# Small products of a recurrent stage in one run per unit, sample products on the whole array, and a prompt stage whose first loads are asked for earlier

## The chip, the cores and the metric

The kernel runs on one core of one Trainium2 chip. The metric is the time of one execution in microseconds (us) on the device; of the kernel before it is 2415.64 us, the median of three runs.

## The reference

One inference step of a trunk layer for 2048 prompt tokens and 32 sample tokens (8 sequences of 4), 1024 channels wide. A norm and one input projection feed two branches; both are gated, projected back, merged and added to the input. Branch A is sparse attention (8 query heads, 2 key heads of 64) with a compressed, a selected and a sliding-window part. Branch B is a gated linear recurrence over 4 heads of 128 x 128 state, and it is what the change is about:

```
G = cumsum(log f)                      # per channel, within a chunk
A[t,s] = sum_d q[t,d] exp(G[t,d]-G[s,d]) k[s,d]   for s <= t
o[t]   = (q[t] exp(G[t])) S + sum_s A[t,s] v[s]
S      = exp(G_last) S + sum_s (k[s] exp(G_last-G[s]))^T v[s]
o      = o / rms(o) * norm_g * silu(z)
```

The sample tokens run the same recurrence from eight given states.

## The kernel before, in words

The kernel is one program whose instructions a scheduler orders on each engine, over the whole program, by what the code's order and the readiness of operands suggest; a block under `high_priority()` is taken ahead of what it would otherwise stand behind. The stages follow each other in the code: loading and compressing the prompt (to about 400 us), sample attention (to 600), the recurrent stage `hgrn` (640 to 1296), `attention_setup` and the preparation of the first two prompt blocks (to about 1386), and the prompt's attention blocks with the output projection (to the end). A generator of projection products is spread between them: `fill(ns)` issues so many ns of it, by a credit, after every step of a stage. Its products are those of L375 and L456 and, last, L435 (the gate columns, spread as 512- and 272-token products, written out to `mb_d` by L441); they are f16 and whole-array.

`hgrn` treats 32 units, eight chunks of 256 tokens by 4 heads, each chunk as two halves j of 128 tokens. A decay matrix within 128 tokens is made of products at five distances (`LEVELS` 64, 32, 16, 8, 4) and one for the nearest tokens. `factors` makes for each distance a factor tile X0 to X4 (a subtraction on DVE at L728, abs and exp on ACT at L729 and L730, two multiplies on POOL at L731 and L732), and the tiles Bk, Bq, Kd, Xo. `scores` multiplies them on PE in f32, by parts of the array: L751 one 64 x 64 product of X0 and two 32 x 32 of X1, L755 four 32 x 32 each of X2, X3, X4 and of Bk with Bq, for each j, 38 products a unit, into a PSUM tile `p4` for each j (two buffers). ACT and DVE gather them into AT (L758 to L766). `values` then makes the state's addend (L774), the outputs (L778 from AT, L780 from the state S) and the next S (L783, L785). `gate_out` scales, transposes (L659), gates and stores (L667, L668) four units at a time. `sample_heads` is put in as one step after each unit from the seventh on: 4 heads with tiles of 32 rows (products at L806, L811, L813, L818, L828, L838). A product in f32 shows as two records in the trace.

After the last unit `attention_setup` opens the pool `pc` (selected-key operands), makes scales, and loads `szs`, gates the sample outputs on DVE (L1410 to L1412) and stores them (L1413, L1414). Then `prompt_phase` opens its pools, asks for block 0's operands (L1500 to L1503), its window's keys (L1480 to L1485) and the selected keys, and prepares two blocks of two groups each: maxima (L1567), bias rows (L1445), scores (L1575, L1576), values (L1461 to L1464), selection on DVE (L1591 to L1599) and a transpose (L1603). All these loads are issued by the SP queue in order. A `pfill(2850.0)` after each step puts projection products between the steps. Pools on the right side of SBUF are stacked: a pool opened after another was closed takes its memory.

## Time and profile before

| | |
|---|---|
| median of three runs (lowest, highest) | 2415.64 us (2414.82, 2417.95) |
| the profiled execution | 2413.94 us |
| its span, first to last instruction | 2412.2 us |
| PE busy | 2279.5 us, 94% |
| DVE, ACT, POOL busy | 1533.5, 1182.3, 1021.4 us |
| mean granted TensorE clock | 0.980 of full speed |
| chain that ended last, by engine | PE 72%, DVE 11%, DMA 6%, ACT 4% |

An engine's busy time is the time in which at least one of its instructions is under way. PE is pipelined: many small products overlap, so the count of records times the mean of one is more than the busy time, and the distance of one start to the next is what a product costs. A run of like products is one row (`x20`); its length runs from the first start to the last end. `PEclk` is the granted TensorE clock in tenths or as a share of full speed. `[... <-DMA x]` behind a row is the engine's idle time before it and what ended it. The chain of waits and the waits of PE say which engine is waited for.

### The profile page before, as it was taken

Reading aid. Unit: us, or ns where it says so; the run is one execution under the profiler, and the core shown is the slowest. Engines: PE = TensorE matmul, PEld = TensorE weight load, DVE = VectorE, ACT = ScalarE, POOL = GpSimd, SP = SyncE. Lnnn points to the kernel's source line nnn. Section 1 sums busy time; section 2 is a strip of 40 time slices with the busy share of each in tenths; the row PEclk is TensorE's granted clock in tenths of the full one; section 3 lists DMA queues with packets and bytes.
Section 4 is the critical chain, followed back from the end, with each engine's and each line's share of the span. In section 5 each row is a group of like instructions: output and inputs, shape, how many; then the busy total and the mean of one; then the engine's idle time right before and its main releaser. Section 6 shows DMA issues by size and latency. Waiting matters only on the chain.

```text
span 2412.2 us, 56868 instructions
## 1 busy us (share of the span) xinstructions
PE 2279.5 (94%) x22181; PEld 1545.1 (64%) x22181; DVE 1533.5 (64%) x4088; ACT 1182.3 (49%) x2606; POOL 1021.4 (42%) x1184
## 2 busy tenths in 40 slices
PE   6999998999899998999989799899999999999998
PEld 5898775555685555556656456667677666665765
DVE  7555554756613689777774356768677677767543
ACT  5544332521422266555663256356556566667663
POOL 0000102242500056555550035356656567777764
PEclk9999999999999999999999899999999999999999
DMA  6643313676842443333332533432222221211121
GB/s 205 178 127 117 127 71 107 230 257 219 256 125 75 152 142 112 115 111 116 117 102 93 141 121 95 111 85 80 63 85 83 61 63 43 72 50 48 52 58 43
DMA packets 276109, 271.89 MB, mean 113 GB/s; under 512 B 102296, under 2 KB 246176, under 8 KB 268416
## 3 DMA queue, kind: packets, MB, share of 16 engines
q1 hardware_dynamic: 267328, 230.51, 31.2%
q0 software_dynamic: 8512, 37.75, 4.7%
q8 instruction: 174, 2.85, 0.5%
q14 instruction: 95, 0.78, 0.1%
HBM read 184.66 MB, written 87.74 MB: 113 GB/s over the span
## 4 chain that ended last, share of the span: by engine, by line
PE 72%; DVE 11%; DMA 6%; ACT 4%; issue 3%; SPq 2%; POOL 1%; ACTq 0%; POOLq 0%; DVEq 0%
PE ps L375 17%; PE ps L1809 7%; PE ps L1777 7%; PE ps L456 7%; PE ps L435 5%; PE st L1666 3%; PE st L1656 3%; PE mx L1536 3%; PE ph L969 2%; DVE X L728 2%; PE po L1461 2%; PE po L1462 2%; PE po L1464 2%; DMA wraw<-in_w_in_dram 1%; PE pt L952 1%
## 5 line engine op out<-in xcount | busy, mean ns | idle before, releaser
L1455 POOL TENSOR_TENSOR Pl<-P,Ph 128x512 f16<-128x512 f32 x444 | 522.1, 1186 | 316.6 <-ACT Ph L1454 178.6
L1453 ACT ACTIVATE P<-st 128x512 f32<-128x512 f32 x444 | 264.8, 597 | 239.8 <-PE st L1666 185.3
L375 PEld LDWEIGHTS <-wh 128*128 128x128 f16 x2240 | 216.0, 98 | 167.8 <-issue 16.2
L1454 ACT ACTIVATE Ph<-st 128x512 f16<-128x512 f32 x444 | 263.1, 595 | 10.5 <-PE po L1462 8.3
L375 PE MATMUL ps<-xh,wh 128*128 128x512 f16 (+1 forms) x1120 | 229.6, 342 | 4.7 <-DVE row L388 3.5
L375 PE MATMUL ps<-xh,wl 128*128 128x512 f16 (+1 forms) x1120 | 232.9, 343 | 0.0
L375 PE MATMUL ps<-xl,wh 128*128 128x512 f16 (+1 forms) x1120 | 231.7, 341 | 0.5 <-issue 0.5
L1539 DVE TENSOR_REDUCE mps<-mx 128x1 f32<-128x512 f32 (+3 forms) x320 | 185.8, 602 | 60.3 <-PE mx L1538 29.5
L456 PE MATMUL ps<-wh,xh 128*128 128x256 f16 (+1 forms) x680 | 190.3, 280 | 10.1 <-ACT to L464 4.8
L456 PE MATMUL ps<-wh,xl 128*128 128x256 f16 (+1 forms) x680 | 189.2, 279 | 4.1 <-DVE xl L341 4.1
L456 PE MATMUL ps<-wl,xh 128*128 128x256 f16 (+1 forms) x680 | 189.9, 279 | 0.0
L1461 PEld LDWEIGHTS <-Ph 128*128 128x128 f16 x1776 | 139.8, 98 | 39.5 <-ACT Ph L1454 5.2
L375 PEld LDWEIGHTS <-wl 128*128 128x128 f16 x1120 | 109.4, 99 | 83.1 <-issue 6.1
L456 PEld LDWEIGHTS <-xh 128*128 128x128 f16 x1360 | 131.1, 99 | 32.4 <-issue 7.7
L1462 PEld LDWEIGHTS <-Ph 128*128 128x128 f16 x1776 | 128.4, 97 | 32.6 <-issue 0.5
L697 POOL TENSOR_TENSOR Xo<-Xo,qt 128x256 f32<-128x256 f32 x32 | 33.3, 1041 | 260.7 <-ACT Xo L696 210.0
L1539 DVE TENSOR_REDUCE mpw<-mx 128x1 f32<-128x512 f32 (+3 forms) x224 | 102.8, 482 | 40.5 <-PE mx L1538 40.0
L1777 PEld LDWEIGHTS <-xh 128*128 128x128 f16 x1280 | 105.0, 98 | 32.7 <-issue 7.1
L731 POOL TENSOR_TENSOR X<-X,kt 128x128 f32<-128x128 f32 x160 | 91.5, 574 | 65.4 <-ACT X L730 63.0
L1464 PEld LDWEIGHTS <-Pl 128*128 128x128 f16 x1776 | 94.2, 97 | 25.9 <-POOL Pl L1455 8.8
L1461 PE MATMUL po<-vs,Ph 128*128 128x65 f16 x1088 | 105.5, 192 | 2.6 <-DVE otmp L1553 2.0
L1462 PE MATMUL po<-vs,Ph 128*128 128x64 f16 x1088 | 104.8, 193 | 0.0
(528 smaller groups left out, 5824.0 us busy)
## 6 DMA issues: line engine op xcount, KB each, us to landing
wraw<-in_w_in_dram SPq DMA_DIRECT2D x22, 1024.0 KB
xt<-in_x_prompt_dram SPq DMA_DIRECT2D x32, 512.0 KB
ma_d<-row SPq DMA_DIRECT2D x8, 1040.0 KB
out_y_prompt_dram<-xt SPq DMA_DIRECT2D x16, 512.0 KB
sg<-ma_d SPq DMA_DIRECT2D x56, 128.0 KB
sg<-mb_d SPq DMA_DIRECT2D x56, 128.0 KB
q_d<-row SPq DMA_DIRECT2D x4, 1040.0 KB
lf_d<-row SPq DMA_DIRECT2D x4, 1040.0 KB
```

The lines of the kernel that those rows point to most:

```text
L375: mm(ps, l[:, kc], xs(r, t0, n)[:, kc], k == 0, k == 23)
L435: mm(ps, l[:, kc, a * 128:(a + 1) * 128], xs(r, t0, n)[:, kc], k == 0, k == 23)
L456: mm(ps, x, w[:, kc], k == 0, k == 23)
L1453: ac.activation(P[:n], ps, AF.Exp, scale=1.0 / QS)
L1454: ac.activation(ph[:n], ps, AF.Exp, scale=1.0 / QS)
L1455: sub.tensor_sub(pl[:n], P[:n], ph[:n])
L1461: mm(po[:, r, :w], ph[:n, rs[r]], v[:n, :w], first and r == 0, False)
L1462: mm(po[:, r, :64], ph[:n, rs[r]], v[:n, w:w + 64], False, False)
L1464: mm(po[:, r, :w], pl[:n, rs[r]], v[:n, :w], False, last)
L1539: ve.tensor_reduce(mp_[:, r, c:c + 1], pmf[:, :n], axis=AX.X, op=OP.max)
L1777: mm(X["ps"], w[:, kc, cs], os_[o][:, kc], k == 0, k == 11)
L1809: mm(X["ps"], X["y"][y][:, kc, i0:i0 + r], W["o", kc // 4][w][:, kc % 4, cs], k == 0, k == 23)
```

## The change

Three things are changed in the code.

1. `scores` now issues all products of a unit, both halves j, in one loop under `high_priority()`, into one PSUM tile for both halves. Within a half X4 comes first, then Bk with Bq, X3, X2, X0, X1. The 64 x 64 product of X0 is written as two pieces of 32 columns by 64 tokens, so a unit has 40 products, all 32 wide, where it had 38.
2. The sample tiles with 32 rows or 32 columns are replaced by zeroed tiles of 128 (eight memsets on POOL when the stage begins), of which the first 32 are written. The products read the whole tiles. The last transpose of the samples becomes a product with the first 32 columns of the identity.
3. `prompt_phase` is a generator. It is opened before `attention_setup`: its pool `pu`, the memsets of XD and REP, block 0's loads and the window's loads stand ahead of `attention_setup` in the program; `pc` is opened later, in the first `load_keys`, and the PSUM pools after the generator is taken up again. The prompt's main part is then called from inside.

```diff
@@ -656,7 +656,10 @@
                 for j in range(nt):
-                    pe.transpose(pt[:, j * 128:j * 128 + r], o_sb[:r, j], ident[:r, :r])
+                    if r == 128:
+                        pe.transpose(pt[:, j * 128:j * 128 + r], o_sb[:, j], ident)
+                    else:
+                        mm(pt[:, j * 128:j * 128 + r], o_sb[:, j], ident[:, :r], True, True)
...
+            WIDE = {}
             def common(h, t0, n, L):
                 sfx = "" if n == NC else "_s"
                 def new(name, bufs=2):
+                    if n != NC and name in ("Bk", "Kd"):
+                        return WIDE[name][:, :n]
                     return hp.tile([128, n], F32, name=name + sfx, bufs=bufs if n == NC or name == "E" else 1)
@@ -739,25 +746,34 @@
+                p4 = pa.tile([128, 4, 128], F32, name="p4")
+                first = set()
+                for j in range(NJ):
+                    prod = []
+                    for li, (l, r) in reversed(list(enumerate([(x, x) for x in u["Xs"][2:]] + [(u["Bk"], u["Bq"])]))):
+                        for b in range(4):
+                            bs = slice(j * 128 + 32 * b, j * 128 + 32 * b + 32)
+                            prod.append((b, p4[32 * b:32 * b + 32, 2 * j + 1, 32 * li:32 * li + 32], l[:, bs], r[:, bs]))
+                    prod = prod[4:8] + prod[:4] + prod[8:]
+                    for li, L in enumerate(LEVELS[:2]):
+                        X = u["Xs"][li][:, j * 128:(j + 1) * 128]
+                        for s0 in range(0, 128, 2 * L):
+                            for c0 in range(s0, s0 + L, 32):
+                                prod.append((c0 // 32, p4[c0:c0 + 32, 2 * j, s0 + L:s0 + 2 * L], X[:, c0:c0 + 32], X[:, s0 + L:s0 + 2 * L]))
+                    with tc.high_priority():
+                        for b, o, l, r in prod:
+                            mm(o, l, r, b not in first, True)
+                            first.add(b)
                 u["AT"] = []
                 for j in range(NJ):
-                    tj = slice(j * 128, (j + 1) * 128)
-                    p4 = pa.tile([128, 4, 128], F32, name="p4")
-
-                    near = p4[:, 1].rearrange("p (l t) -> p l t", l=4)
-                    for li, L in enumerate(LEVELS[:2]):
-                        X = u["Xs"][li][:, tj]
-                        for s0 in range(0, 128, 2 * L):
-                            mm(p4[s0:s0 + L, 0, s0 + L:s0 + 2 * L], X[:, s0:s0 + L], X[:, s0 + L:s0 + 2 * L], li == 0 or s0 == 64, True)
-                    for li, (l, r) in enumerate([(x, x) for x in u["Xs"][2:]] + [(u["Bk"], u["Bq"])]):
-                        for b in range(4):
-                            bs = slice(j * 128 + 32 * b, j * 128 + 32 * b + 32)
-                            mm(near[32 * b:32 * b + 32, li], l[:, bs], r[:, bs], li == 0 and b == 3, True)
+                    near = p4[:, 2 * j + 1].rearrange("p (l t) -> p l t", l=4)
-                    ac.activation(AT[:64, 2:], p4[:64, 0, 64:].rearrange("p (b t) -> p b t", t=32), AF.Copy)
+                    ac.activation(AT[:64, 2:], p4[:64, 2 * j, 64:].rearrange("p (b t) -> p b t", t=32), AF.Copy)
...
+                        ac.activation(AT[s0:s0 + 32, s0 // 32 + 1], p4[s0:s0 + 32, 2 * j, s0 + 32:s0 + 64], AF.Copy)
...
             def sample_heads():
+                def zeros(name, shape):
+                    t_ = hc.tile([128] + shape, F32, name=name)
+                    gp.memset(t_, 0.0)
+                    return t_
+                for nm in ("Bk", "Kd", "oT"):
+                    WIDE[nm] = zeros(nm + "_s", [128])
+                v_, AT_, o_, kd_, vm_ = zeros("vs_", [128]), zeros("ATs", [32]), zeros("o_s", [1, 128]), zeros("kd_s", [128]), zeros("vm", [4, 128])
                 for h in range(4):
                     G, qt, kt, Bq, Bk, Xo, Kd, eG = common(h, 2048, 32, 4)
-                    v = hp.tile([32, 128], F32, name="vs_")
+                    v = v_[:32]
...
                     pb = po.tile([128, 512], F32, name="pk")
-                    mm(pb[:32, :32], Bk, Bq, True, True)
-                    AT = hp.tile([32, 32], F32, name="ATs")
+                    mm(pb[:, :32], WIDE["Bk"], Bq, True, True)
+                    AT = AT_[:32]
                     ve.tensor_mul(AT, pb[:32, :32], lmf[:32, 3])
...
-                    mm(ov, v, AT, True, False)
+                    mm(ov, v_, AT_, True, False)
...
-                    oT = hp.tile([128, 32], F32, name="oT")
+                    oT = WIDE["oT"][:, :32]
...
                     pt = po.tile([128, 512], F32, name="pk")
-                    pe.transpose(pt[:32, :128], oT, ident)
-                    o_sb = hp.tile([32, 1, 128], F32, name="o_s")
+                    pe.transpose(pt[:, :128], WIDE["oT"], ident)
+                    o_sb = o_[:32]
...
-                    gate_out(o_sb, load_z(h, 2048, 32), y, 1, 32, h, 2048)
+                    gate_out(o_, load_z(h, 2048, 32), y, 1, 32, h, 2048)
...
-                    pe.transpose(pk[:32, 0], Kd, ident)
-                    kd = hp.tile([32, 128], F32, name="kd_s")
+                    pe.transpose(pk[:, 0], WIDE["Kd"], ident)
+                    kd = kd_[:32]
...
-                        vm = hp.tile([32, 4, 128], F32, name="vm", bufs=1)
+                        vm = vm_[:32]
...
                         pu = po.tile([128, 512], F32, name="pu").rearrange("p (a b) -> p a b", a=4)
-                        mm(pu, kd, vm, True, True)
@@ -1346,16 +1371,16 @@
     def attention_setup(st, a):
-        pc_ = st.enter_context(tc.tile_pool(name="pc", bufs=1, side="right"))
         KA, KB, V = a["KA"], a["KB"], a["V"]
-        a["sel0"] = pc_.tile([128, 16, 32], F32, name="h_sel0")
-        for g in range(2):
-            KA["s", g] = pc_.tile([100, NP], F16, name=f"kas{g}")
-            KB["s", g] = pc_.tile([128, NP], F16, name=f"kbs{g}")
-        V["s"] = pc_.tile([128, 16, 2, 129], F16, name="vs16")
         def load_keys(t0, t1):
             if t0 == 0:
+                pc_ = st.enter_context(tc.tile_pool(name="pc", bufs=1, side="right"))
+                a["sel0"] = pc_.tile([128, 16, 32], F32, name="h_sel0")
+                for g in range(2):
+                    KA["s", g] = pc_.tile([100, NP], F16, name=f"kas{g}")
+                    KB["s", g] = pc_.tile([128, NP], F16, name=f"kbs{g}")
+                V["s"] = pc_.tile([128, 16, 2, 129], F16, name="vs16")
                 sy.dma_start(a["sel0"], A["c_sel0"].rearrange("p (t j) -> p t j", j=32))
...
@@ -1420,8 +1445,6 @@
     def prompt_phase(a, st, pfill, state, sw):
         KA, KB, V, TB, TQ = a["KA"], a["KB"], a["V"], a["TB"], a["TQ"]
         pu = st.enter_context(tc.tile_pool(name="pu", bufs=2, side="right"))
-        pst = st.enter_context(tc.tile_pool(name="pst", bufs=2, space=PSUM, side="right"))
-        pmx = st.enter_context(tc.tile_pool(name="pmx", bufs=3, space=PSUM, side="right"))
@@ -1620,15 +1643,19 @@
         def open_block(i):
             units[i] = [loads(ORDER[i], g, i % 2) for g in range(2)]
+        open_block(0)
+        want(ORDER[0])
+        yield
+        pst = st.enter_context(tc.tile_pool(name="pst", bufs=2, space=PSUM, side="right"))
+        pmx = st.enter_context(tc.tile_pool(name="pmx", bufs=3, space=PSUM, side="right"))
         state["env"]["tp"] = lambda: pmx.tile([128, 4, 128], F32, name="mx").rearrange("p a b -> p (a b)")
         wc = sw.enter_context(tc.tile_pool(name="wc", bufs=3))
         state["env"]["piece"] = lambda: wc.tile([128, 512], F32, name="piece")
         for i in range(2):
-            open_block(i)
             if i == 0:
-                want(ORDER[0])
                 a["load_keys"](0, 512)
             else:
+                open_block(1)
                 a["load_keys"](512, NP)
             c = [prep(units[i][g], ORDER[i], g) for g in range(2)]
...
-        return main
+        main()
...
@@ -2004,10 +2031,13 @@
         along(hgrn(), 1250.0)
         fill(0, ("z", 2))
         fill(350.0)
+        prompt = prompt_phase(att, s2, fill, state, sw)
+        next(prompt)
         along(attention_setup(s2, att), 15000.0)
         fill(0, ("ma", 6))
         sb.close()
-        prompt_phase(att, s2, fill, state, sw)()
+        for _ in prompt:
+            pass
```

On PE in the middle of the recurrent stage of before, at 956 to 960 us of the trace: p_11089 and p_11127 are the `p4` tiles of one unit's halves, X_11042, X_11048, X_11054, X_11060 and X_11066 its X0 to X4.

```order
L751 MATMUL p_11089<-X_11042 64x64
L778 MATMUL ov<-v,AT_8650 128x128
L780 MATMUL ov<-S_10027,Xo 128x128
L778 MATMUL ov<-v,AT_8652 128x128
L751 MATMUL p_11089<-X_11048 32x32 x2
L755 MATMUL p_11089<-X_11054 32x32 x4
L755 MATMUL p_11089<-X_11060 32x32 x4
L755 MATMUL p_11089<-X_11066 32x32 x4
L755 MATMUL p_11089<-Bq,Bk 32x32 x4
L751 MATMUL p_11127<-X_11042 64x64
L751 MATMUL p_11127<-X_11048 32x32 x2
```

The same unit after the change, where X_10849 to X_10873 are X0 to X4:

```order
L375 MATMUL ps<-xl_127,wh 128x512
L767 MATMUL p_10890<-X_10873 32x32 x4
L767 MATMUL p_10890<-Bq,Bk 32x32 x4
L767 MATMUL p_10890<-X_10867 32x32 x4
L767 MATMUL p_10890<-X_10861 32x32 x4
L767 MATMUL p_10890<-X_10849 32x64 x2
L767 MATMUL p_10890<-X_10855 32x32 x2
```

The first of the unit's products stood ahead of two of `values`' lines and a 64 x 64 product stood in the middle of the 32 x 32 ones; now the rows of the first half are followed by the same six of the second half, with nothing between, and then by whole-array products (L660, L790).

On SP at the end of the recurrent stage of before, from the last stores of the recurrent output (L668) on; qs, qc and qb are block 0's operands, h_sel the table that selection on DVE adds to, kas and kbs the selected keys:

```order
L668 DMA obl_d<-gl 128x256
L441 DMA mb_d<-piece 128x272
L1409 DMA szs<-sz_d 64x8x32
L1359 DMA h_sel_16055<-in_c_sel_dram 128x512
L1361 DMA kas_16056<-ksx_d_89 64x512
L1362 DMA kbs_16057<-ksx_d_89 128x512
L1364 DMA kas_16056<-in_c_kblk_dram 36x2048
L1413 DMA oah_d<-OSh 64x8x32
L1414 DMA oal_d<-OSl 64x8x32
```

After the change, on the same queue, the end of the window's loads and what follows:

```order
L1508 DMA vw_16123<-vwx_d 128x2x258
L1434 DMA szs<-sz_d 64x8x32
L1523 DMA qs<-qh_d 64x4x128
L1523 DMA qc<-qh_d 64x4x128
L1523 DMA qb<-qh_d 64x4x128
L1438 DMA oah_d<-OSh 64x8x32
L1439 DMA oal_d<-OSl 64x8x32
L1524 DMA qc<-tc_d_87 32x512
L1526 DMA qb<-ql_d 64x4x128
L1384 DMA h_sel_16513<-in_c_sel_dram 128x512
L1386 DMA kas_16514<-ksx_d_89 64x512
```

The ten loads of block 0 and the fourteen of its windows (24 rows, L1523 to L1508) stand directly behind the last stores of the recurrent output, ahead of szs; three loads of block 1 have come ahead of oah; h_sel stands behind all of them.

On PE where block 0's preparation begins, before (kbc and kac are the compressed keys):

```order
L1567 LDWEIGHTS qc
L1567 MATMUL mx<-kac_6516,qc 128x32
L1575 LDWEIGHTS kbc_6518
L1575 MATMUL st<-qb,kbc_6518 128x512
L435 LDWEIGHTS wh
L435 MATMUL ps<-xh_121,wh 128x512
```

and after:

```order
L1590 LDWEIGHTS qc
L1590 MATMUL mx<-kac_6516,qc 128x32
L1598 LDWEIGHTS kbc_6518
L1598 MATMUL st<-qb,kbc_6518 128x512
L1590 LDWEIGHTS qc
L1590 MATMUL mx<-kac_6525,qc 128x32
```

The projection products of L435 that stood between the steps of the two groups no longer stand there. Counted along PE's order, before has 265 of them (169 of 512 tokens, 96 of 272) up to the recurrent stage's last product, 125 (119 and 6) from there to its last transpose, 114 (24 and 90) from there to block 0's first product, and 72 of 512 from there to the first weight transpose (L188) behind the two preparations. After has 450 (288 and 162), 123 (93 and 30), 3 and 0. Behind that point both have the same 384. Changes of the part of the array that is used (whole, 64 wide, 32 wide, 32 rows) are 429 before and 170 after: 89 fewer from the whole array to a narrower form, 92 fewer that leave a 32-wide form, 62 fewer that leave a 64-wide one, 16 fewer that leave 32 rows.

## Rows read from the trace of the kernel before

**Rows 1.** Windows: us, PE, PEld, DVE, ACT, POOL busy, PEclk, DMA share, GB/s.
```profile
840.00:1060.00 220.00, 200.37 (x2144) 124.69 (x2143) 188.82 (x541) 134.88 (x467) 135.36 (x220) 0.95 0.38 123
...
1339.00:1366.00 27.00, 20.58 (x118) 9.46 (x116) 6.84 (x33) 4.68 (x8) 2.31 (x2) 0.87 0.61 164
```
**Rows 2.** Waits of PE, 640 to 1290 us: total, times, longest.
```profile
PE ov L659 <- DVE o_sb L656: 10.7, 3, 5.0
PE p L751 <- POOL X L732: 3.5, 1, 3.5
...
PE pk L739 <- POOL Kd L703: 0.2, 1, 0.2
```
**Rows 3.** Timeline of PE in the recurrent stage: start, length, instruction.
```profile
956.87 0.33 PE L751 MATMUL p<-X 128*64 128x64 f32 x2
957.13 0.49 PE L778 MATMUL ov<-v,AT 128*128 128x128 f32 x2
957.45 0.39 PE L780 MATMUL ov<-S,Xo 128*128 128x128 f32 x2
957.68 0.39 PE L778 MATMUL ov<-v,AT 128*128 128x128 f32 x2
957.99 0.22 PE L751 MATMUL p<-X 128*32 128x32 f32 x2
...
958.07 0.34 PE L755 MATMUL p<-X 128*32 128x32 f32 x20
...
958.78 0.37 PE L755 MATMUL p<-X 128*32 128x32 f32 x16
959.08 0.49 PE L780 MATMUL ov<-S,Xo 128*128 128x128 f32 x2
```
**Rows 4.** Timeline of PE from the last recurrent product to the prompt's blocks.
```profile
1295.91 0.38 PE L780 MATMUL ov<-S,Xo 128*128 128x128 f32 x2
...
1323.27 0.38 PE L659 MATMUL ov<-ident,o_sb 128*128 128x128 f32 x2
...
1366.82 0.35 PE L1567 MATMUL mx<-kac,qc 96*128 96x24 f16 x8
...
1379.61 0.42 PE L188 MATMUL mx<-ident,wmx 128*128 128x128 f32 x1
...
1385.86 1.89 PE L435 MATMUL ps<-xh,wh 128*128 128x512 f16 x8
1387.58 1.67 PE L435 MATMUL ps<-xl,wh 128*128 128x512 f16 x7
```
**Rows 5.** Groups by form, PE, 840 to 1300 us: busy, mean ns, idle before.
```profile
L838 PE MATMUL pu<-vm,kd_s 32*128 32x512 f32 x16 | 8.9, 634 | 7.5 <-DVE vm L836 3.4 <-DVE own L764 2.3 <-DVE own L762 1.1
```
**Rows 6.** Timeline of SP's queue behind the last transpose.
```profile
1326.88 0.66 SPq L1409 DMA_DIRECT2D szs<-sz_d  x1
...
1330.39 0.63 SPq L1413 DMA_DIRECT2D oah_d<-OSh  x1
...
1333.36 0.60 SPq L1500 DMA_DIRECT2D qs<-qh_d  x1
...
1341.06 0.57 SPq L1480 DMA_DIRECT2D kw<-in_c_wone_dram  x1
...
1344.88 0.43 SPq L1480 DMA_DIRECT2D kw<-in_c_wone_dram  x1
```
**Rows 7.** Timeline of DVE: gating of the samples and block 0's selection.
```profile
1329.57 0.42 DVE L1410 TENSOR_TENSOR OS<-OS,szs 64x256 f32<-64x256 f32 x1 [4.50 <-DMA szs<-sz_d]
...
1350.95 0.24 DVE L1591 SCALAR_TENSOR_TENSOR im<-mx,h_sel 128x32 f32<-128x32 f32 x1
...
1352.89 0.19 DVE L1599 TENSOR_TENSOR repp<-repp,im 128x32 f32<-128x32 f32 x1
```
**Rows 8.** One source line on POOL: instructions, ns min/median/max, first and last start.
```profile
L732 POOL TENSOR_TENSOR X<-X,qt x160: 443/456/2500, 641.3 to 1263.8; 128x128 f32<-128x128 f32 x160
```

More of the change, by code (lines that the diff above doesn't have):

```diff
@@ L759, in scores @@
                     for s0 in (0, 64):
-                        ac.activation(AT[s0:s0 + 32, s0 // 32 + 1], p4[s0:s0 + 32, 0, s0 + 32:s0 + 64], AF.Copy)
+                        ac.activation(AT[s0:s0 + 32, s0 // 32 + 1], p4[s0:s0 + 32, 2 * j, s0 + 32:s0 + 64], AF.Copy)
                     own = hp.tile([128, 32], F32, name="own")
@@ L837, in sample_heads @@
                         pu = po.tile([128, 512], F32, name="pu").rearrange("p (a b) -> p a b", a=4)
-                        mm(pu, kd, vm, True, True)
+                        mm(pu, kd_, vm_, True, True)
                         for b in range(4):
```

## The prediction

> **What bounds the kernel now.** I read the page's busy shares first: PE is busy 94% of the span, so the first question for each part is how much PE time it removes and whether something else takes the place. Then the windows of the two stages that the change touches. In the middle of the recurrent stage PE is busy 200.4 of 220 us and DVE 188.8 of 220 [rows 1]: PE bounds it, DVE stands close behind. In the preparation of the first blocks PE is busy 20.6 of 27 us and the granted clock is 0.87 [rows 1]: there it is latency, not work. The waits of PE within the recurrent stage are 16 rows, from 10.7 us down to 0.2, 34 us together; the largest is for DVE's scaled outputs, the one for a factor of POOL 3.5 us, once [rows 2]. Last, the timelines, for what a small product costs, and for the chain from the last recurrent product to the first block's maxima [rows 3, 4, 6, 7].
>
> **Part 1, the small products in one run.** What a product costs is the distance from its start to the next start. Sixteen 32-wide records stand in a row of 0.37 us; one record alone lasts about 0.2 (two take 0.22), so the last starts some 0.17 after the first, at 958.95, and the records are 0.011 apart. The next product, whole-array, starts at 959.08: leaving the 32-wide form cost 0.13, against 0.01 for one more record, so 0.12 [rows 3]. Entering: two whole-array products take 957.68 to 957.99, 0.31, when a 32-wide one follows, and 957.45 to 957.68, 0.23, when a whole-array one does: 0.08 [rows 3]. A 64 x 64 product (two records) takes 956.87 to 957.13, 0.26, its leaving included [rows 3].
> Counted along PE's order, 89 enterings go (89 x 0.08 = 7.1), 92 leavings of the 32-wide form (92 x 0.12 = 11.0), and 64 products of 64 x 64 (64 x 0.26 = 16.6), for which 128 pieces of two records come. No row shows a 32-wide piece over 64 tokens. At the spacing of the 32-wide records they cost 256 x 0.011 = 2.8; as dear as 64-wide records (0.13 each) they would cost 33, and at nothing 0. I take 2.8, the nearest in width of weights. That is 7.1 + 11.0 + 16.6 - 2.8 = 31.9 us of PE less; with the dear pieces 2, with free ones 35. A further 0.09 (957.13 to 957.45 takes 0.32 against 0.23) is lost by the first f32 whole-array product behind a change; where f16 products follow I see no such row, so I count 0 and keep 154 x 0.09 = 14 for the range.
>
> **Part 2, the samples.** Sixteen leavings of the 32-row form go, at no more than 0.09 each: 1 us. The dearest group, L838, is 8.9 us in all [rows 5]; as whole-array products it may lose 1 us, and cannot lose more than the 8.9; it could gain some if the wider arrays cost more weight loading, which I bound by the same 1 us. The eight memsets lie on POOL, which has 85 of 220 us free even at its fullest [rows 1]. I take 2 us for part 2: 34 us of PE work less in all.
>
> **Where it goes.** The scheduler has put other work in the place. Up to the last recurrent product 119 more L435 products of 512 tokens and 66 more of 272 stand in the order. Eight of 512 tokens take 1385.86 to 1387.58, 0.215 each [rows 4]; by columns one of 272 is an estimated 0.114. So 119 x 0.215 + 66 x 0.114 = 33.1 us come into the stage. PE's work there stays the same within a microsecond. I take the stage's waits (34 us) as unchanged too: the chains of DVE and ACT that end them are the same instructions. The last recurrent product then stays at about 1296 us, and the gain is what leaves the stretch behind it.
>
> **The stretch behind.** Before, from the last recurrent product (1295.91) to the weight transpose behind both preparations (1379.61) it is 83.7 us [rows 4]. The L435 products in it are 215 of 512 and 96 of 272: 215 x 0.215 + 96 x 0.114 = 57.2 us; 26.5 us is everything else. After, up to the last transpose stand 93 and 30: 23.4 us, plus about 1 us of transposes: 24.4. Behind it stand three, so nothing covers the preparation any more, and its chain is the time:
> - last transpose to SP's next free issue, 1323.27 to 1326.88: 3.6 [rows 4, 6]. This is where the first load now stands; before, it was issued at 1333.36, so it is asked for 6.5 us earlier.
> - The ten loads of block 0 take SP 1333.36 to 1341.06, 7.7; seven window loads 1341.06 to 1344.88, 3.8, and there are fourteen: 7.6 [rows 6].
> - Only then szs: 1326.88 to DVE's product at 1329.57, 2.7; to the store, 1330.39, 0.8; from there to the first free load, 1333.36, 3.0 [rows 6, 7]. The pool that holds h_sel takes the place of the pool that held those store tiles, so h_sel is issued behind their landing, 25.4 us behind the transpose. I give its landing the 2.7 of szs: 28.1.
> - Block 0's selection waits for h_sel: 1350.95 to the end at 1353.08 is 2.1 for one group, 4.2 for two [rows 7]: 32.3. Everything ahead of it in block 0 (maxima, scores, values) finds its loads landed long before and is covered.
> - Block 1's chain behind it, 1366.82 to 1379.61: 12.8 [rows 4], and 1 for the transposes: 46.
> The sum of the stretch is 24.4 + 46 = 70.4 against 83.7: -13.3 us. So 33.8 us of products left the stretch, and 20.5 us of what they covered came to light. The change that asks for the loads earlier is thus one that makes the last of them later. In the rest of the program both orders are alike.
>
> **Sum.** 2413.94 (the profiled execution; its span is 2412.2) - 0.9 in the stage - 13.3 = 2399.7. That execution lies 1.7 us under the median of 2415.64, so the median to expect is 2401.5; I say 2402.
>
> **The rivals.**
> - All arrives (R1). Block 0's selection does not wait for h_sel, or the wait is covered, so the stretch loses its 57.2 - 23.4 us of products and nothing comes in their place: 2413.9 - 0.9 - 33.8 + 1.7 = 2381. For it: SP issues a load in 0.6 us and the queue could be shorter than I count. Against: the six rows of SP's order between szs and h_sel.
> - DVE takes over the stage (R2). In 840 to 1060 it has 31 us free of 220, and the waits of PE name it first [rows 1, 2]. The new order holds the products of a unit until all are there; if the chains behind it grow the waits by a third, 11 us, the time is 2401.5 + 11 = 2412. It is no change.
> - The run waits for the last factor (R3, slower). The first product was of X0; it is now of X4, which POOL finishes four factors later: each costs two multiplies of 0.46 us, so 4 x 2 x 0.46 = 3.7 us [rows 8]. All of PE's queue stands behind it: projections, values, the next transposes. If POOL's lead over a unit's first product is spread evenly over 0 to 10 us, a start 3.7 us later waits 3.7 x 3.7 / 20 = 0.7 us on average, 32 units 22 us: 2401.5 + 22 = 2423. It decides from 0.42 us a unit (13.3 / 32). For it: DVE, whose subtraction starts each factor, is the fullest of the others. Against: the waits on POOL in the whole stage are few, the largest 3.5 us once, and the factors are made one unit ahead.
> - Weights that do not overlap (R4). Twenty 32-wide records in 0.34 us [rows 3] say that weight loads run under the products of other parts of the array. Were each record to take its full 0.2 us, the 128 records more would cost 26 us and the pieces' 13.8 us of gain would go: 2401.5 + 40 = 2441. The Trainium skill, "TensorE: Matmul & The Clock Gate", section "Part 3: Packing small matmuls — row/col tiling", has a rule of this kind: a weight load overlaps products under way only when the row group differs, and all these products use all 128 rows. By that rule this rival would be the forecast; the row of twenty speaks against it.
>
> **How the numbers follow.** Forecast 0.52, with a range of its own of 2391 to 2411 (the pieces' price up, the f32 returns down, and 5 us on the chain either way). R1 0.12, R2 0.20, R3 0.14, R4 0.02. A measurement of this kernel can tell about 0.2%, 4.8 us, from no change. Faster: the forecast but for 0.02 of it, and R1: 0.62. Same: R2 but for 0.02, and that 0.02: 0.20. Slower: R3, R4 and R2's upper end: 0.18. The range of 8 in 10 leaves out R1's lower part, R4 and R3's upper half: 2384 to 2421.
>
> **What would show it.** Right: the last recurrent product within 5 us of 1296; in the run of a unit's eighty records no whole-array product and about 0.9 us; PE's waits in the stage near 34 us; behind the last transpose some 46 us to the weight transpose, in which PE is mostly idle and DVE's first selection ends an idle time on h_sel. Wrong: waits of L767 for POOL's X of over 10 us (R3); waits for DVE up by 10 (R2); the first selection waiting for PE and not for a DMA (R1); 32-wide pieces 0.1 us apart (the dear pieces).

## The result: 0.84% slower

The changed kernel takes 2439.88 us, the median of four runs (2436.4 to 2440.7), the kernel before 2416.8 on the same chip: ratio 1.0084, interval 1.0065 to 1.0103 (the two medians alone give 1.0095, inside the interval). The forecast was 2402, and the time lies outside its range of 2384 to 2421. The span of the profiled execution is 2434.6 us against 2412.2, 22.4 more, and it divides so:

| stretch | before | after | difference |
|---|---|---|---|
| stage: first transpose of Kd to last recurrent product | 657.7 | 688.9 | +31.2 |
| from there to the first weight transpose (L188) behind the preparations | 83.6 | 69.3 | -14.3 |
| from there to the end | 1032.6 | 1038.0 | +5.4 |

The second line was forecast at -13.3. The first was forecast at -0.9.

**The profile after.** Windows of the changed kernel (us, PE, PEld, DVE, ACT, POOL busy, PEclk, DMA share, GB/s), to be read beside [rows 1]:

```profile
840.00:1060.00 220.00, 196.80 (x2172) 126.25 (x2171) 186.87 (x516) 132.71 (x450) 119.37 (x207) 0.94 0.38 123
1060.00:1296.00 236.00, 216.03 (x2265) 135.40 (x2264) 173.59 (x491) 126.79 (x426) 117.66 (x196) 0.95 0.34 108
...
1352.00:1397.00 45.00, 15.28 (x99) 7.64 (x98) 15.77 (x73) 8.04 (x14) 5.44 (x9) 0.55 0.53 138
```

Before, the second of these windows read:

```profile
1060.00:1296.00 236.00, 225.31 (x2279) 143.69 (x2277) 163.79 (x503) 128.75 (x443) 111.71 (x186) 0.99 0.33 105
```

In the stage PE is busy for a smaller share than before (216.0 against 225.3 of 236 us in the second window) and its clock is lower (0.95 against 0.99). In the last window, the preparation without cover, PE works 15 of 45 us.

PE's waits in the stage of the changed kernel (line, waited for: total, times, longest), against [rows 2]:

```profile
PE ov L660 <- DVE o_sb L656: 7.7, 3, 6.2
PE pu L863 <- DVE own L778: 6.7, 3, 3.4
PE ps L375 <- DVE row L397: 5.3, 3, 3.0
PE p L767 <- DVE own L780: 5.2, 2, 4.2
PE ov L794 <- DVE zt L665: 4.9, 3, 3.0
PE p L767 <- POOL X L739: 3.6, 6, 1.2
```

There are 16 such rows, as before. Their sum is 49.4 us, 36.8 of it for DVE; before it was 34.2, with 28.4 for DVE. The wait for the factors (X) is small.

A unit's run of products on PE's timeline, against [rows 3]:

```profile
1046.56 0.63 PE L375 MATMUL ps<-xl,wh 128*128 128x272 f16 x4
1047.12 0.27 PE L767 MATMUL p<-X 128*32 128x32 f32 x8
...
1047.26 0.51 PE L767 MATMUL p<-X 128*32 128x32 f32 x31
...
1047.66 0.49 PE L767 MATMUL p<-X 128*32 128x32 f32 x23
1048.09 0.41 PE L662 MATMUL ov<-ident,o_s 128*128 128x32 f32 x2
```

Eighty records take 1047.12 to 1048.09, 0.97 us, one leaving included. Over the whole stage the next record starts 0.007 us after a 32-token one (median; the mean is 0.011) and 0.021 us after a 64-token one. So the pieces over 64 tokens are dearer than the others, but far from the 0.13 that the prediction feared.

The stretch behind the stage on PE, against [rows 4]:

```profile
1327.19 0.39 PE L796 MATMUL ov<-S,Xo 128*128 128x128 f32 x2
...
1351.61 0.38 PE L660 MATMUL ov<-ident,o_sb 128*128 128x128 f32 x2
...
1359.44 0.27 PE L1590 MATMUL mx<-kac,qc 96*128 96x32 f16 x4 [6.80 <-DMA qc<-tc_d]
...
1396.59 0.42 PE L188 MATMUL mx<-ident,wmx 128*128 128x128 f32 x1
```

SP's queue there, against [rows 6], and then DVE, against [rows 7]:

```profile
1355.19 0.66 SPq L1523 DMA_DIRECT2D qs<-qh_d  x1
...
1369.22 0.61 SPq L1434 DMA_DIRECT2D szs<-sz_d  x1
...
1372.62 0.59 SPq L1438 DMA_DIRECT2D oah_d<-OSh  x1
...
1375.43 0.41 SPq L1384 DMA_DIRECT2D h_sel<-in_c_sel_dram  x1
```

```profile
1371.79 0.42 DVE L1435 TENSOR_TENSOR OS<-OS,szs 64x256 f32<-64x256 f32 x1 [0.18 <-DMA szs<-sz_d]
...
1378.71 0.42 DVE L1614 SCALAR_TENSOR_TENSOR im<-mx,h_sel 128x32 f32<-128x32 f32 x2 [5.60 <-DMA h_sel<-in_c_sel_dram]
```

The chain is the one the prediction laid out: h_sel is issued 23.8 us behind the last transpose (25.4 worked out), DVE idles 5.6 us for it, and the weight transpose comes after 45.0 us (46).

**Where the stage's time went.** For every record of PE in the stage I took the time to the start of the next record, counted the part in which nothing was under way as idle, and summed by kind (us):

| kind | before | after | e13, after again | e15, no priority | e5, no priority | e6, less fill |
|---|---|---|---|---|---|---|
| L375, L456 (same products in all) | 430.4 | 437.6 | 435.9 | 431.6 | 431.3 | 429.4 |
| L435 | 48.4 | 84.3 | 83.6 | 48.2 | 47.1 | 43.5 |
| small products | 56.9 | 33.3 | 33.9 | 44.4 | 43.5 | 34.5 |
| values, transposes, others | 68.8 | 65.4 | 65.5 | 68.3 | 68.2 | 69.2 |
| samples | 18.5 | 19.0 | 17.9 | 17.0 | 19.0 | 17.6 |
| idle | 34.7 | 49.3 | 49.0 | 41.9 | 39.4 | 61.2 |
| sum | 657.7 | 688.9 | 685.8 | 651.4 | 648.7 | 655.4 |
| of it, PE work at the lower clock level (1.2 GHz) | 24.5 | 56.3 | 50.8 | 28.9 | 25.6 | 36.5 |

Before to after: the moved L435 products cost 35.9, the small products give 23.6 and the rest of the recurrence 2.9, idle grows by 14.6, and L375 and L456, the same products, take 7.2 more.

The last line of the table tells what the clock has in this. At the lower of its two levels a product takes twice its time: from one 512-token product of L375 to the next it is 0.427 us there and 0.216 at the upper level (2.4 GHz), in both traces. So half of the work done at the lower level, 12 us before and 28 after, is lost. The sums bear this out: in the changed kernel, e13 and e1, whose orders in the stage are alike, L375 and L456 take 437.6, 435.9 and 432.5 us, and with half of their lower-level time taken off they take 419.3, 419.3 and 419.8. So the 31.2 us of the stage are 33.6 for the moved products at full clock, -32.8 for the forms (small products, the rest of the recurrence, samples, and 4 us on L375 and L456), 14.6 of idle and 15.9 of clock. The last figure varies: three traces of the stage as it was before (before, e2, e9) lose 10 to 16 us to the clock, the three of the changed one 20 to 28.

### The profile page after: what moved, and what is told of

It is laid out like the page before. It is cut to its first block, busy times and chain, and to the rows that moved or that the text cites. A ratio compares the mean times of both kernels' runs of the same rounds, so it can differ in the third digit from the quotient of the medians.

```text
span 2434.6 us, 57060 instructions
## 1 busy us (share of the span) xinstructions
PE 2266.3 (93%) x22313; PEld 1544.4 (63%) x22313; DVE 1550.1 (64%) x4088; ACT 1180.8 (49%) x2606; POOL 1012.2 (42%) x1192
## 4 chain that ended last, share of the span: by engine, by line
PE 69%; DVE 13%; DMA 7%; ACT 4%; issue 3%; SPq 2%; POOL 1%; another core or an unknown queue 0%; POOLq 0%; ACTq 0%; DVEq 0%
PE ps L375 14%; PE ps L1836 7%; PE ps L456 7%; PE ps L1804 6%; PE ps L435 6%; PE st L1693 3%; PE mx L1559 3%; PE st L1683 3%; DVE X L735 3%; PE ph L994 2%; PE po L1484 2%; DMA wraw<-in_w_in_dram 2%; PE po L1487 2%; PE po L1485 2%; PE pt L977 1%
## 5 line engine op out<-in xcount | busy, mean ns | idle before, releaser
L375 PEld LDWEIGHTS <-wh 128*128 128x128 f16 x2240 | 221.2, 100 | 177.7 <-issue 22.0
L375 PE MATMUL ps<-xh,wh 128*128 128x512 f16 (+1 forms) x1120 | 233.1, 346 | 8.3 <-DVE row L397 5.3
L375 PE MATMUL ps<-xl,wh 128*128 128x512 f16 (+1 forms) x1120 | 233.3, 343 | 0.4 <-issue 0.4
L375 PE MATMUL ps<-xh,wl 128*128 128x512 f16 (+1 forms) x1120 | 233.5, 344 | 0.0
L1562 DVE TENSOR_REDUCE mps<-mx 128x1 f32<-128x512 f32 (+3 forms) x320 | 185.8, 602 | 59.9 <-PE mx L1559 29.3
L456 PE MATMUL ps<-wh,xh 128*128 128x256 f16 (+1 forms) x680 | 191.9, 282 | 13.2 <-ACT to L464 8.0
L456 PE MATMUL ps<-wh,xl 128*128 128x256 f16 (+1 forms) x680 | 191.1, 282 | 4.1 <-DVE xl L341 4.1
L456 PE MATMUL ps<-wl,xh 128*128 128x256 f16 (+1 forms) x680 | 191.7, 282 | 0.0
L375 PEld LDWEIGHTS <-wl 128*128 128x128 f16 x1120 | 110.9, 100 | 81.6 <-issue 3.0
L456 PEld LDWEIGHTS <-xh 128*128 128x128 f16 x1360 | 133.7, 100 | 36.1 <-issue 9.4
L1562 DVE TENSOR_REDUCE mpw<-mx 128x1 f32<-128x512 f32 (+3 forms) x224 | 102.4, 481 | 40.3 <-PE mx L1561 39.6
L1804 PEld LDWEIGHTS <-xh 128*128 128x128 f16 x1280 | 105.3, 98 | 34.7 <-issue 10.8
L1683 PE MATMUL st<-qb,kbs 128*128 128x512 f16 x272 | 103.2, 379 | 2.1 <-ACT Ph L1477 1.9
```

Of the source, the lines that this page charges most:

```text
L375: mm(ps, l[:, kc], xs(r, t0, n)[:, kc], k == 0, k == 23)
L456: mm(ps, x, w[:, kc], k == 0, k == 23)
L1562: ve.tensor_reduce(mp_[:, r, c:c + 1], pmf[:, :n], axis=AX.X, op=OP.max)
L1683: mm(ps, kb, flat(u["b"]), True, False)
L1804: mm(X["ps"], w[:, kc, cs], os_[o][:, kc], k == 0, k == 11)
```

## The experiments

Ratios are against the kernel before in the same comparison. Chips differ (the stage begins at 624 us on some, 638 on others), so times are compared within one comparison, and across comparisons only stage lengths and ratios.

**One part at a time (e1 to e4).** The edits are the diff's hunks of the parts named.

> Parts 1 and 2 of the change without part 3 (prompt stage opened as before). PE's order up to the stage's end is that of the changed kernel, so the last recurrent product should come at 1327 us again, 31 later than before, under every theory. Theory A (part 3 makes the table h_sel late and uncovers some 20 us of the preparation, as the prediction worked out): the stretch from there to the weight transpose behind the preparations, 69 us in the changed kernel, is about 50, and the time about 2420. Rival B (part 3 does nothing, the preparation is as long whoever opens it): 2440. Rival C (the loads asked for earlier did help): 2446.

> Part 3 alone on the kernel before. The last recurrent product stays at 1296 us. Theory A (h_sel issued behind 24 loads): the selection waits for it, the chain behind the last transpose is some 46 us where it was 56 with its projection products in it, of which about 31 us are still there and are covered: the stretch of 83.7 us becomes about 74, the time 2407. Rival B (no effect): 2417. Rival C (the late table is not covered by the products, it only adds): 2425 or more.

> Part 1 alone. The scheduler then puts still more projection products into the recurrent stage than in the changed kernel: 497 us of them at full clock against 460 before and 488 in the changed kernel. Theory A (the stage is held by the chains of DVE and ACT between a unit's products; what is put in adds to it, and the changes of form saved on PE go into waits): last recurrent product at 1333 to 1337 us. Rival B (PE's work bounds it, 31 us of it went with the forms): 1302 us. Rival C (the sample part is what lengthened the stage): 1296 to 1305. The time of the whole by theory A: about 2420, the stretch behind losing the 43 us of products that moved.

> Part 2 alone, samples on the whole array. The order of the rest is nearly that of before. Theory A: 16 changes of form from 32 rows fewer, -1 to -2 us, the last recurrent product at 1294 to 1297, the time 2415. Rival C (the sample part is what lengthened the stage, by its waits on zeroed tiles or by wider weights): last recurrent product at 1305 or later, the time 2425 or more.

| | ratio (interval) | last recurrent product | from there to L188 |
|---|---|---|---|
| e1, parts 1 and 2 | 1.0082 (1.0056 to 1.0109) | 1327.1 | 69.7 |
| e2, part 3 | 0.9987 (0.9975 to 0.9999) | 1295.0 | 81.2 |
| e3, part 1 | 1.0042 (1.0029 to 1.0055) | 1329.1 | 63.8 |
| e4, part 2 | 1.0035 (1.0020 to 1.0050) | 1299.9 | 86.6 |

Part 1 lengthens the stage, as theory A of e3 said, 4 us short of its number (1333 to 1337 expected). For part 3 rival B holds in e1: without it the stretch is the same. PE in e1:

```profile
1351.37 0.38 PE L660 MATMUL ov<-ident,o_sb 128*128 128x128 f32 x2
1366.65 0.27 PE L1592 MATMUL mx<-kac,qc 96*128 96x32 f16 x4 [14.24 <-DMA qc<-tc_d]
...
1396.71 0.42 PE L188 MATMUL mx<-ident,wmx 128*128 128x128 f32 x1
```

SP's queue in e1:

```profile
1355.68 0.62 SPq L1384 DMA_DIRECT2D h_sel<-in_c_sel_dram  x1
```

The first block starts 7 us later than in the changed kernel and ends level: in e1 h_sel is early and block 0's loads are late, in the changed kernel it is the other way round. What uncovers the preparation is that its projection products have gone, by part 1. Part 3 alone is worth 0.13%, a third of what theory A gave. Part 2 alone costs 0.35%. That is the time of rival C (2425.74 us; 2425 or more expected), but not its reason: the last recurrent product comes at 1299.9, not at 1305 or later. In e4's one trace PE has 40.8 us of work in the stage at the lower clock level; the traces of before, e2 and e9, with the old samples, have 20 to 31. Some 5 to 10 us would come from that.

**Without the priority (e5, e15, e17).**

```diff
-                    with tc.high_priority():
-                        for b, o, l, r in prod:
+                    for b, o, l, r in prod:
```

> The changed kernel without the high_priority() around the run of a unit's products; part 1's layout, parts 2 and 3 stay. The products again stand in 131 pieces and the projection products stay behind the stage (450 us of them in it, 488 in the changed kernel). Theory D (PE waits for DVE's work, and by priority the run only stands early: in the changed kernel the first small product comes 2.9 us after the last factor, before it came 9 us after, but DVE and ACT take 24 us instead of 10 to make AT of it): taking the priority away brings the last recurrent product back to 1296 to 1302 us and the time to 2410 to 2420. Rival W (the run waits for the last factor and holds PE's queue): the same direction, but the waits of PE for POOL's X, 3.6 us in the changed kernel, would have to be what goes. Rival L (the layout of 40 pieces in one tile is what costs): the stage stays at 1320 or more.

> The changed kernel again, for a trace and a ratio on the chip of the next three runs. Ratio 1.006 to 1.010 and a stage of 686 to 692 us, as on the first chip (688.9), if the loss is the program's; 1.000 to 1.004 if it is that chip's.

> e5 beside the changed kernel on one chip. Theory (the priority is what costs: it stands products early that nobody uses earlier and draws projection products into the stage): ratio 0.7 to 1.2% below e13's, at 0.996 to 1.001 against before. If e5's 0.9963 was its chip's, the upper end.

> e5 and e15 once more, in five rounds, since the kernels without the priority stood between 0.9963 and 1.0012 on different chips. If its gain is the program's: ratio 0.996 to 0.998 on any chip. If it is to be had only where the stage begins early (624 us on the chips of e5 and e15, 638 on the others): 0.999 to 1.002 where it begins at 638.

e5 0.9963 (0.9946 to 0.9980), e15 0.9973 (0.9958 to 0.9988), e17 0.9970 (0.9960 to 0.9981), on three chips; e13, the changed kernel on e15's chip, 1.0086 (1.0056 to 1.0116). Within the changed kernel the priority costs 1.1%, and the change without it is 0.3% faster than the kernel before. e17's stage begins at 639 us, so the gain is not that of an early start. The run stands in pieces again; PE in e15, with a whole-array product (L746) among a unit's products and L660 waiting for DVE between others:

```profile
1001.34 0.26 PE L766 MATMUL p<-X 128*32 128x32 f32 x6
1001.54 0.44 PE L746 MATMUL pk<-ident,Kd 128*128 128x128 f32 x2
...
1002.03 0.25 PE L766 MATMUL p<-X 128*32 128x32 f32 x5
1002.93 0.44 PE L660 MATMUL ov<-ident,o_sb 128*128 128x128 f32 x2 [0.65 <-DVE rsz L243]
1003.30 0.47 PE L766 MATMUL p<-X 128*32 128x32 f32 x23
```

The small products cost 44.4 us instead of 33.9, and yet the stage is 34 us shorter: 35 of L435 stay behind it, idle is 7 less, and the clock takes some 11 less (28.9 us at the lower level against 50.8). The products that stay behind cost little there, since they cover the preparation: from the last recurrent product to L188 e15 takes 79.6 us, e13 69.2.

From the traces, the means over units 5 to 32: before, a unit's first small product starts 9.0 us after POOL ends the last factor, and AT is complete 22.8 us after it; in the changed kernel 2.9 and 27.4; in e15 4.1 and 24.7. The priority makes the products earlier and what they are for later. But AT's time does not decide the stage: it is later than before in e15 too, whose stage is shorter than before's.

**Less fill (e6).** `along(hgrn(), 900.0)` for 1250.0 in the changed kernel.

> The changed kernel with 900 instead of 1250 ns of projection credit a step in the recurrent stage; by the order no L435 product is left in the stage (449 us of projections, 488 in the changed kernel), and all stand behind the preparations. Theory P (the stage is PE's work plus waits that do not depend on it, so what was moved in was paid in full): the last recurrent product at 1327 - 36 = 1291 us or earlier, waits of PE still near 50. Theory D+ (the chain over DVE holds the stage; the products only fill its waits): last product at 1310 or later, the waits growing by 20 or more. The whole time tells little here, since the products are done later.

Stage 655.4 us, 33.5 less than the changed kernel's, for 40.8 us of L435 taken out, with idle 12 more and some 10 us less of clock. Up to the last four units idle is the same (39.9 us; 40.4 in the changed kernel), which is theory P: there the products moved in were paid in full. The 12 us more of idle are in the last four units.

e5, on the same chip, has as many projections in the stage (450 by the order, 449 here) and no priority, is 6.7 us shorter although its small products cost 9 more, and has 39.4 us of idle against 61.2. Most of that difference is not the priority's. The products of e6 are used up earlier: the last one in the stage starts at 1243.8 us, 37 us ahead of the stage's end, and in the last four units there are 8 where e5 has 208. Windows of these units (us, PE, PEld, DVE, ACT, POOL busy, PEclk, DMA share, GB/s), e5 and then e6:

```profile
1215.00:1273.00 58.00, 52.54 (x609) 34.84 (x608) 38.26 (x125) 29.95 (x111) 25.55 (x44) 0.94 0.26 84
```

```profile
1237.00:1280.00 43.00, 21.64 (x376) 17.24 (x363) 34.39 (x101) 25.70 (x104) 26.61 (x44) 0.68 0.21 61
```

Ahead of them e6 idles 39.9 us and e5 34.0: some 6 us are left that the priority may cost in idle by itself. PE's waits in e5, where by rival W the wait for X (3.6 us in the changed kernel) would have to be what goes (it falls by 1.6 us):

```profile
PE pk L746 <- POOL Kd L710: 5.8, 4, 2.2
PE ov L660 <- DVE o_sb L656: 5.2, 4, 3.2
...
PE p L766 <- POOL X L739: 2.0, 3, 1.0
```

The time of e6 (1.0048) says little: its L435 products are done in the prompt's blocks.

**A joined gathering (e7, e14, e8, e11, e18).** AT of both halves is one tile; ACT's copies and DVE's products are issued once for both (the line of the last copy stays one for each j):

```diff
-                for j in range(NJ):
-                    own = hp.tile([128, 32], F32, name="own")
-                    ve.tensor_mul(own, near[:, 3], lmf[:, 3])
...
+                own = hp.tile([128, NJ, 32], F32, name="own")
+                ve.tensor_mul(own, p4v[:, :, 1, 96:], lmf[:, 3][:, None, :].to_broadcast([128, NJ, 32]))
...
```

> The changed kernel with the gathering of a unit's products joined over both halves: 3 copies on ACT for 6, 6 instructions on DVE for 10; PE's order hardly changes (489 us of projections in the stage). The four DVE instructions less a unit are 32 x 4 x 0.2 = 26 us less of DVE's queue. Theory D (PE waits for DVE): last recurrent product 10 to 20 us earlier than 1327, PE's waits in the stage at 30 to 40 us, the time 2420 to 2430. Rival P (PE's work and the clock, DVE's load does not matter): 1324 to 1330, 2437.

> e7 beside the changed kernel on one chip. Theory D (PE waits for what DVE and ACT have to do for a unit): stage 10 to 16 us shorter than in e13, ratio 0.4 to 0.7% below e13's. Rival (e7's gain was its chip's): stage and ratio as e13 within 0.15%.

> Parts 1 and 3 without the priority, the samples as before, the gathering joined as in e7: the version to which theory D points. By theory D the stage keeps before's order of projections and DVE has 26 us less: last recurrent product at 1275 to 1290 us, the time 2390 to 2408. By rival P (DVE does not matter) it is part 1's and part 3's sum without priority: 1296, 2410 to 2417.

> e5 with the gathering joined over both halves (26 us less of DVE's queue and three copies less a unit on ACT). Theory D, that PE waits for DVE also without the priority: the stage 5 to 12 us shorter than in e5, ratio 0.990 to 0.994. Rival: without the priority DVE's load is covered: ratio 0.996 as e5.

> e11 beside e17 on one chip: the joined gathering without the priority. Theory D: 0.3% or more below e17. Rival (without the priority DVE's work for a unit is covered, and the joined gathering, which can begin only when both halves are done, even lengthens it): equal within 0.15%, or above e17.

With the priority it gains: e7 1.0008 (0.9993 to 1.0023); e14 1.0005 (0.9987 to 1.0024) beside e13's 1.0086, the stage 674.7 against 685.8, idle 42.2 against 49.0. PE's waits for DVE fall from 37.0 to 23.8 us there, and those for POOL rise from 4.8 to 12.7.

Without the priority it depends on part 2. With part 2 it loses: e11 1.0012 (0.9996 to 1.0027), and e18 1.0015 (1.0003 to 1.0026) beside e17's 0.9970, its stage 663.1 against 653.7, with 32.0 us of idle behind small products against 17.3. Without part 2 it gains: e8 0.9968 (0.9951 to 0.9986), where the same kernel with the old gathering (e10, e16, below) has 1.0012 and 0.9997, its stage 651.3 against 659.2 and 661.6. So theory D, that PE waits for the amount of DVE's work, foretells e7, e14 and e8 and fails in e11 and e18. That the joined form has to wait for both halves does not explain e18. From the last factor on, its first half of AT is complete 1.6 us later than in e17 and its second 1.7 us earlier, and in e8, which gains, both come as in e18 (23.2 and 23.5 us; 23.3 and 23.7). The cause of the loss stays open.

It also bounds what was said of the priority: with the joined gathering, taking it away brings nothing (e14 1.0005, e11 and e18 1.0012 and 1.0015, on different chips).

**The samples and the layout (e9, e10, e16, e12).** e10 and e16 are parts 1 and 3 without the priority, e12 part 1 without it, e9 the kernel before.

> The kernel before, unchanged, for a trace from the chip on which the next three run. The stage from the first transpose of Kd to the last recurrent product should be 655 to 660 us as in the first trace (657.7), whatever the chip's time for what stands ahead of it; if it is 10 us shorter, the stage's lengths of two chips cannot be compared.

> Parts 1 and 3 without the priority, samples as before. Against e5 (the same with part 2, ratio 0.9963): if part 2 costs what it cost alone (0.35%), the ratio is 0.993; if it costs only by how it shifts an order near its limit, the ratio is 0.995 to 0.998. By theory D the stage is 645 to 652 us, as in e5.

> e10 beside e15 on one chip: they differ by part 2 alone. If part 2 costs what it did alone (0.35%), e16 is 0.2 to 0.5% below e15; if its cost alone came from one order that it happened to bring about, they are equal within 0.2% or e16 is above.

> Part 1's layout alone, without the priority: 40 pieces of 32 columns in one tile where there were 38 products in two. By the sum of forms: 64 products of 64 x 64 gone (the 13.8 us of the prediction), the other changes hardly fewer (126 pieces of run for 125): the stage 8 to 14 us shorter than before, ratio 0.994 to 0.997. Rival L (the layout costs, since nothing of the first half can be gathered before the tile's last product): ratio 1.000 or more.

e9's stage is 660.8 us. e10 1.0012 (0.9995 to 1.0030), e16 0.9997 (0.9981 to 1.0013) beside e15's 0.9973, e12 1.0001 (0.9987 to 1.0016). Part 2, which cost 0.35% alone, gains 0.24% here (the intervals overlap at their ends), with hardly a change in the samples' own time (17.0 against 19.0 us). Of the 10.2 us by which e16's stage is longer than e15's, some 6.5 are clock (42.3 against 29.3 us at the lower level).

Part 1's layout alone saves 12 us of small products (44.8 against 56.9), and stage (657.1 us) and time stay. Its expectation of a stage 8 to 14 us shorter failed. The ratio is rival L's, but not by its reason: the first half's AT comes 21.1 us after the last factor in e12 and 21.6 before. L375 takes 6.7 us more, and it is clock: 22.4 us of it are at the lower level, 9.8 before.

Of the kernels with part 1 but without the priority, those that have one of part 2 and the joined gathering gain 0.3%; those that have neither or both do not. The stages of those that gain have 25.5 to 39.6 us of PE work at the lower clock level (e5, e15, e17, e8), the others 41.6 to 51.3 (e10, e16, e12, e11, e18). Why one order has more of it than another, no run shows.

## Why the prediction was wrong, step by step

- **Forms: right, 32.8 at full clock for 34.** As they stand in the table, small products, values, transposes and samples fell from 144.2 to 117.7 us; another 4 us at full clock lie in L375 and L456, and the rest is hidden by the lower clock. The 64-token pieces cost about twice what was taken (0.021 us a record, some 2.6 us more in all). Part 2's 2 us did not appear in the samples as the table has them (18.5 to 19.0).
- **Products moved into the stage, 33.1: right.** 33.6 at full clock.
- **"I take the stage's waits (34 us) as unchanged too": this step failed.** They went to 49.3. The reason given, that the chains' instructions are the same, leaves out that their order is not: the run's priority changes what stands ahead of what on PE, DVE and ACT. Without the priority the loss is gone (e5, e15, e17). On one chip idle goes from 49.0 to 41.9 with it (e13, e15), about half of the way back; the rest stays with the other edits.
- **The clock was not in the sum; this term was put at nothing without a reason.** The lower level holds for 56 us of PE's work in place of 25, which is 15.9 us, as much as the waits. More idle alone does not tell it: e6 has 61.2 us of idle and 36.5 at the lower level, e4 35.9 and 40.8. What sets it here stays open.
- **The stretch behind, -13.3: right, -14.3**, and its chain term by term. But that the late h_sel, and so part 3, is what brings 20 us to light was wrong: e1, without part 3, has the same stretch. Either order of the loads ends level once nothing covers them.
- **"In the rest of the program both orders are alike":** +5.4 us; e13's stretch is 1034.8, e1's 1035.9, so some of it is one execution's. Its cause stays open.
- **The rivals.** R4's 2441 is within 2 us of the measured time, and R3's 2423 is next, both by mechanisms that did not happen. The run starts 2.9 us behind the last factor and PE waits for POOL's X 3.6 us in all, so R3 is out. R4 is excluded by eighty records in 0.97 us. The Trainium skill, "TensorE: Matmul & The Clock Gate", section "Part 3: Packing small matmuls — row/col tiling", lets a weight load overlap products under way only where the row group differs. All loads of the run use the same 128 rows, so the measurement decides against that rule here. R2 had a mechanism that happened, waits for DVE: it priced the waits at 11 us where 14.6 came, 8.4 of them for DVE, and had no clock. R1 did not happen.
- **The chances.** What spoke most for a gain, fewer changes of form at measured prices, was true. The chances had no rival in which the clock falls.

## What to carry to other kernels

A sum of what an engine does less is not yet a time. Here its products came out within 2 us, and 30 us of waits and of lower clock that stood in no term turned the gain into a loss: give both a term and a range of their own. Products moved into a stage cost their full time there and give back behind only what they did not cover (33.6 us in, 14.3 out). A priority given to one step of a scheduled program reorders every engine that feeds or follows it, and draws fill out of the places it covered: try the edit with and without it. Here the edit without its priority is 0.3% below the kernel before on three chips; parts 1 and 3 with the joined gathering (e8) are level with it. Edits whose sign turns with what stands beside them, as part 2 and the joined gathering do here, can't be priced one at a time.

## What was not expected of the hardware

Twenty 32-column weight loads with all 128 rows, 0.11 us each by their records, run under each other so that a record costs 0.011 us, and one over 64 tokens 0.021. The two clock levels made the same projection products of the stage take between 429.4 and 437.6 us in six traces, and cost the stage of the changed kernel 28 us. One program's ratio held within 0.1% on three chips, while the kernel before took 2401, 2402, 2415 and 2417 us on different ones.
